# A hybrid decoder block on one core: causal mask added on VectorE with the row's extreme, input stage and scan reordered

## The chip, the cores and the metric

One core of a Trainium2 chip. The metric is the device time of one execution in microseconds (us), given as the median of several runs. Engines are named as in the profile: PE (TensorE, matrix products), PEld (its weight loads), DVE (VectorE), ACT (ScalarE), POOL (GpSimd), SP (SyncE, which here issues most DMA transfers, in a queue of its own that keeps their order).

## What is computed

One decoder layer for 512 tokens of width 1024, in f32. One projection of the normalised input feeds a Mamba-2 scan (SSD, 32 heads in 4 groups, chunks of 128) and a latent attention (16 heads); both are gated and merged. A cross-attention to 256 memory rows and a mixture of 32 experts follow. Of the parts that the change touches the reference reads:

```python
u = rms_norm(h, norm_mix)                     # x * rsqrt(mean(x*x) + 1e-6) * gain
z, xbc, dt_raw, q_a, c_kv, k_rope, gate_ssd, gate_mla = split_cols(u @ w_in, IN_SPLITS)
...
y = ssd_chunked_scan(xh, dt, a, bm, cm)
y = y + d_skip[:, None] * xh
...
sc = einsum('bqhd,bkhd->bhqk', qi, k) * 96 ** -0.5      # queries in blocks of 128
sc = where(kpos[None, :] <= qpos[:, None], sc, -inf)    # causal
o = einsum('bhqk,bkhd->bqhd', softmax(sc), v)
```

## The kernel before

Everything is one function, `block`. Each f32 product with a weight is made of three: the activations lie in SBUF as a high part and a rest (`uh`, `ul`), each weight tile of 128x1024 is split on its arrival into `WHt` (a copy on ACT, L149) and `WLt` (a subtraction on DVE, L150), and `mm3` (L118 to L126) issues the products of high and high, of the rest with `WHt`, and of high with `WLt`, each in 8 steps of 128 rows: 24 PE instructions with 512 columns per output tile. The weights come through `wraw` (L131) in SP's queue into a tag with two buffers.

Input stage (L202 to L255, in a `manual_schedule`, where instructions stay in the order in which they are written): four token tiles `xt[t]` of 128x1024 are loaded; PE is kept busy by 50 identity products (`keep_warm`); ACT squares each tile and sums it (L231); DVE makes the reciprocal roots for two tiles at a time (`mean_rsqrt`, L79 to L109, an integer start and three steps); the tiles are scaled in place (L234 and L243 on DVE, L237 and L244 on ACT); the narrow weights `wd` are split (L241, L246); PE transposes all 32 blocks (L251); ACT and DVE make `uh` and `ul` out of PSUM (L253, L254). Then PE starts with the narrow product (L121, k by k) and the latent projections.

All else is put in order by a list scheduler in the tile framework; pools of buffers (tag `tmp` with four, PSUM tags A and B with four banks each) hold instructions back until a buffer is free. SP's queue holds in order the weight loads, two strided loads of `d_skip` into `dsk` (L313, 64x16 elements of 4 bytes each), the load of the rope table's first two columns `fr` (L570), the rows of the convolution, `dtb` and `ea` (L112).

The scan: `project(g)` gives six output tiles of the projection for group g, with a convolution on each (`conv`, L378 to L389: one ACT and three DVE operations, a tanh, a product). `scan(g)` (L413 to L478) is a generator: one step with the scores of the chunks and the transposes of B, four with transposes of `y` (L431) and products of states (L440), and four for pairs of heads, whose decay rows come back from DRAM as broadcasts (`ac_d`). `drive(a, b, na, nb)` interleaves two generators, na steps of a to nb of b:

```python
    for g in range(3):
        drive(scan(g), project(g + 1), 9, 6)
    drive(scan(3), gate(0), 9, 5)
```

The attention runs in pairs of heads. `stage1` makes query and key, high and rest; `stage2` (L695 to L718) makes the scores of 4 query blocks for both heads in three products each (L706 to L708), a fourth product `identb` x `mQ` (L709) adds -1e30 above the diagonal, DVE takes the negated row maximum from PSUM (L711), ACT takes the exponential from PSUM to SBUF with the row sum (L712), DVE normalises (L713, L718). `stage3` transposes the result on PE (L730), `stage4` multiplies with v. A PSUM bank holds one or two score blocks, and the next ones can have it when the exponentials have read it.

## Time and profile before

| | us |
|---|---|
| median of 3 runs | 1193.38 |
| lowest and highest | 1190.51, 1193.88 |
| profiled execution | 1194.35 |
| its span in the trace | 1192.6 |
| PE busy, in 5972 instructions | 1164.2 |
| PE weight loads | 861.9 |
| DVE busy, in 1500 instructions | 730.8 |
| ACT busy, in 1010 instructions | 517.2 |
| POOL busy | 99.6 |

The granted clock of PE over the whole span is 0.992 of full speed. Weight loads overlap with products. Products of PE are pipelined: a row's duration is longer than the step from one to the next, so the cost of an instruction on PE is read from the starts. An idle time stands in square brackets with what ended it.

## The change

Five parts.

1. Input stage: the root is made for each token tile by itself (ACT square with the mean's factor, ACT root with the epsilon as bias, four small DVE operations, the scaling on DVE), and PE's transposes of a tile stand right behind it. The transposition of the gains (`gcol`) moves to the third tile. `qa0`, the first split of latent weights, is taken after the fourth `uh`/`ul`. A root on a constant has ACT load its table at the start; later the exponential of `a_log` needs a load of its own (7 table loads in the program, before 6).
2. `d_skip`: one broadcast load of 128 rows of 32 (`dsr`) behind the rows of the convolution, and two DVE copies, take the place of the two strided loads.
3. `fr` and `perm`, two loads, become one (`frp`, 128x130), late; two tiles of the same tag grow to 130 columns.
4. Scan: both generators are started by a step each before `drive`.
5. Attention: queries are scaled by the negative factor; `hide`, a bf16 tile with 0 and 1e30, is added to the negated scores by one DVE operation that writes the sum to SBUF and keeps its minimum (`tensor_tensor_reduce`); ACT takes the exponential of what lies in SBUF with scale -1. The 64 mask products and `identb` are gone.

```diff
-    for t in range(NT):
-        junk = tmp([128, D], BF, name="junk")
-        A.activation(junk, xt[:, t], AF.Square, accum_out=ss[:, t:t + 1])
-        if t == 1:
-            rs = mean_rsqrt(sb.tile([128, 2], F32, name="va", tag="rsv", bufs=4), ss[:, :2], 2, 1.0 / D, "rx")
-            V.tensor_scalar(xt[:, 0], xt[:, 0], rs[:, 0:1], None, op0=OP.mult)
-    T.transpose(pu[7][:, :n2], rows2[:n2], ident[:n2, :n2])
-    V.tensor_copy(gcol[:, :n2], pu[7][:, :n2])
-    A.activation(xt[:, 1], xt[:, 1], AF.Copy, scale=rs[:, 1:2])
+    rx = const([128, 4, NT], name="rx")
+    epsx = const([128, 1], name="epsx")
+    V.memset(epsx, EPS)
+    A.activation(rx[:, 0, :1], epsx, AF.Sqrt)
     wdh, wdl = wsplit([128, KD, 96])
     wdc = ((0, 0, 64), (64, 48, 16), (80, 32, 16))
+    for t in range(NT):
+
+        q = slice(t, t + 1)
+        rt, y, v, r = (rx[:, i, q] for i in range(4))
+        junk = tmp([128, D], BF, name="junk")
+        A.activation(junk, xt[:, t], AF.Square, scale=1.0 / 32, accum_out=ss[:, q])
+        A.activation(rt, ss[:, q], AF.Sqrt, bias=epsx)
+        V.tensor_scalar(v, ss[:, q], EPS, -0.5, op0=OP.add, op1=OP.mult)
+        V.reciprocal(y, rt)
+        V.tensor_scalar(v, y, v, y, op0=OP.mult, op1=OP.mult)
+        V.tensor_scalar(r, v, 1.5, y, op0=OP.add, op1=OP.mult)
+        V.tensor_scalar(xt[:, t], xt[:, t], r, None, op0=OP.mult)
+        if t == 2:
+            T.transpose(pu[7][:, 384:384 + n2], rows2[:n2], ident[:n2, :n2])
+            V.tensor_copy(gcol[:, :n2], pu[7][:, 384:384 + n2])
+        for d in range(KD):
+            T.transpose(pu[d][:, t * 128:(t + 1) * 128], xt[:, t, d * 128:(d + 1) * 128], ident)
     for o0, i0, n in wdc:
         A.activation(wdh[:, :, o0:o0 + n], wd[:, :, i0:i0 + n], AF.Copy)
-    rs = mean_rsqrt(sb.tile([128, 2], F32, name="vb", tag="rsv", bufs=4), ss[:, 2:], 2, 1.0 / D, "rx")
-    V.tensor_scalar(xt[:, 3], xt[:, 3], rs[:, 1:2], None, op0=OP.mult)
-    A.activation(xt[:, 2], xt[:, 2], AF.Copy, scale=rs[:, 0:1])
     for o0, i0, n in wdc:
         V.tensor_sub(wdl[:, :, o0:o0 + n], wd[:, :, i0:i0 + n], f(wdh[:, :, o0:o0 + n]))
-    it_q = parts(w_in, 0, C_QA, QL, lo=G)
-    qa0 = next(it_q)
-    for t in range(NT):
-        for d in range(KD):
-            T.transpose(pu[d][:, t * 128:(t + 1) * 128], xt[:, t, d * 128:(d + 1) * 128], ident)
     for d in range(KD):
         A.activation(uh[:, d], pu[d], AF.Copy, scale=gcol[:, d:d + 1])
         stt(ul[:, d], pu[d], gcol[:, d:d + 1], f(uh[:, d]), OP.mult, OP.subtract)
+        if d == 3:
+            it_q = parts(w_in, 0, C_QA, QL, lo=G)
+            qa0 = next(it_q)
...
     dsk = const([128, 16], name="dsk")
     ds_ = I["d_skip"]
+    dsr = tmp([128, 16, 2], name="dsr")
+    row_bcast(dsr.rearrange("p j s -> p (j s)"), ds_, 32)
     for s in range(2):
-        nc.sync.dma_start(dsk[s * 64:(s + 1) * 64],
-                          bass.AP(tensor=ds_.tensor, offset=ds_.offset + s, ap=[[0, 64], [2, 16]]))
+        V.tensor_copy(dsk[s * 64:(s + 1) * 64], dsr[s * 64:(s + 1) * 64, :, s])
...
-    for g in range(3):
-        drive(scan(g), project(g + 1), 9, 6)
-    drive(scan(3), gate(0), 9, 5)
+    for g in range(NG):
+        sc, nx = scan(g), project(g + 1) if g < 3 else gate(0)
+        next(sc)
+        next(nx)
+        drive(sc, nx, 8, 5 if g < 3 else 4)
...
-    fr = const([128, 2], name="fr")
-    nc.sync.dma_start(fr, I["freq"][:, :2])
-    perm = sb.tile([128, 128], F32, name="perm", tag="dec")
-    nc.sync.dma_start(perm, I["freq"][:, 2:])
+    frp = sb.tile([128, 130], F32, name="frp", tag="dec")
+    nc.sync.dma_start(frp, I["freq"])
+    fr, perm = frp[:, :2], frp[:, 2:]
...
-    Pq = slot(2, [128, 3, 1280], name="Pq")
+    S2 = slot(2, [128, 4096], name="S2t")
+    Pq = S2[:, :3840].rearrange("p (s n) -> p s n", s=3)
+
+    hide = S2[:, 3840:].bitcast(BF)
+    V.memset(hide[:, :384], 0.0)
+    V.tensor_scalar(hide[:, 384:], mQ, -1.0, None, op0=OP.mult)
...
-    scale = 96 ** -0.5
+    scale = -96 ** -0.5
...
                 T.matmul(dst, Ql[:96, s, qs], Kh[:96, s, :n], start=False, stop=False)
-                T.matmul(dst, Qh[:96, s, qs], Kl[:96, s, :n], start=False, stop=False)
-                T.matmul(dst[:, n - 128:], identb, mQ, start=False, stop=True)
+                T.matmul(dst, Qh[:96, s, qs], Kl[:96, s, :n], start=False, stop=True)
                 mx = sm[:, 0, s, qc:qc + 1]
-                V.reduce_max(mx, dst, axis=AX.X, negate=True)
-                A.activation(P[:, ROFF[qc]:ROFF[qc] + n], dst, AF.Exp, bias=mx, accum_out=sm[:, 1, s, qc:qc + 1])
+                w = P[:, ROFF[qc]:ROFF[qc] + n]
+                V.tensor_tensor_reduce(w, hide[:, 512 - n:], dst, 1.0, 3e38, OP.add, OP.min, accum_out=mx)
+                A.activation(w, w, AF.Exp, scale=-1.0, bias=mx, accum_out=sm[:, 1, s, qc:qc + 1])
```

SP's queue at the start, before (`wr` are weights, `rows` those of the convolution):

```order
L220 DMA wd<-in_w_in_dram 128x8x32 x2
L131 DMA wr<-in_w_in_dram 128x8x256
L313 DMA dsk<-in_d_skip_dram 64x16x1 x2
L570 DMA fr<-in_freq_dram 128x2
L131 DMA wr<-in_w_in_dram 128x8x128
L131 DMA wr<-in_w_in_dram 128x8x256
L131 DMA wr<-in_w_in_dram 128x8x128 x2
L131 DMA wr<-in_w_in_dram 128x8x256 x2
L308 DMA rows<-in_conv_w_dram 96x128
L309 DMA rows<-in_conv_b_dram 24x128
L112 DMA dtb<-in_dt_bias_dram 128x32
L112 DMA ea<-in_a_log_dram 128x32
L131 DMA wr<-in_w_in_dram 128x8x128
```

And now:

```order
L218 DMA wd<-in_w_in_dram 128x8x32 x2
L129 DMA wr<-in_w_in_dram 128x8x256
L129 DMA wr<-in_w_in_dram 128x8x128
L129 DMA wr<-in_w_in_dram 128x8x256
L129 DMA wr<-in_w_in_dram 128x8x128 x2
L129 DMA wr<-in_w_in_dram 128x8x256 x2
L313 DMA rows<-in_conv_w_dram 96x128
L314 DMA rows<-in_conv_b_dram 24x128
L110 DMA dsr<-in_d_skip_dram 128x32
L110 DMA dtb<-in_dt_bias_dram 128x32
L110 DMA ea<-in_a_log_dram 128x32
L129 DMA wr<-in_w_in_dram 128x8x128
```

The loads of `dsk` and `fr` no longer stand between the weight loads; `dsr` stands behind the rows of the convolution. Line numbers differ by some, as the file is longer.

PE at the start of the scan of group 0, before (`pcb` and `pbt` are the scores and the transposes of B, `pxt` the transposes of `y`, `pa` the products of the projection of group 1):

```order
L420 MATMUL pcb<-S8t 128x128 x4
L424 MATMUL pbt<-ident,S8t 128x128 x3
L431 MATMUL pxt<-ident,y_540 128x128
L126 MATMUL pa<-uh,WHt 128x512 x8
L431 MATMUL pxt<-ident,y_540 128x128
L126 MATMUL pa<-ul,WHt 128x512 x2
L431 MATMUL pxt<-ident,y_540 128x128
L126 MATMUL pa<-ul,WHt 128x512 x6
L126 MATMUL pa<-uh,WLt_76 128x512 x8
L431 MATMUL pxt<-ident,y_540 128x128 x3
```

And now:

```order
L426 MATMUL pcb<-S8t 128x128 x4
L430 MATMUL pbt<-ident,S8t 128x128 x3
L124 MATMUL pa<-uh,WHt 128x512 x8
L124 MATMUL pa<-ul,WHt 128x512 x8
L124 MATMUL pa<-uh,WLt_74 128x512 x8
L437 MATMUL pxt<-ident,y_524 128x128 x6
```

The first six transposes of `y` stand together behind 24 products; before, the first came ahead of them all and the second behind 8.

DVE at the scores of one pair of heads, before:

```order
L645 TENSOR_TENSOR WLt_76<-wkv,WHt 128x512 x2
L711 TENSOR_REDUCE sm<-psc 128x1 x8
L713 RECIPROCAL sm<-sm 128x8
L718 TENSOR_SCALAR Pq<-Pq,sm 128x128
L718 TENSOR_SCALAR Pq<-Pq,sm 128x256
```

And now (an operation with an accumulator shows as two instructions, the second reads it):

```order
L657 TENSOR_TENSOR WLt_74<-wkv,WHt 128x512 x2
L723 ISA S2t,sm<-S2t,psc 128x512
L723 ISA sm 128x1
L723 ISA S2t,sm<-S2t,psc 128x384
L723 ISA sm 128x1
L723 ISA S2t,sm<-S2t,psc 128x512
L723 ISA sm 128x1
...
L723 ISA sm 128x1
L725 RECIPROCAL sm<-sm 128x8
L730 TENSOR_SCALAR S2t<-S2t,sm 128x128
```

Eight reductions become eight masked operations with a read each. On PE the same place loses the loads of `identb` and the mask products; from the end of the attention on, the order is the same on all engines.

## Rows read from the trace of the kernel before

**Rows 1.** The page, part 1: busy us (share of the span) xinstructions.
```profile
PE 1164.2 (98%) x5972; PEld 861.9 (72%) x5972; DVE 730.8 (61%) x1500; ACT 517.2 (43%) x1010; POOL 99.6 (8%) x117
```
**Rows 2.** Waits of PE: what for, us in total, times, longest.
```profile
PE pxt L431 <- DVE y L55: 3.0, 1, 3.0
PE pa L126 <- ACT WHt L149: 2.5, 1, 2.5
...
PE pst L440 <- POOL S6t L435: 0.6, 1, 0.6
```
**Rows 3.** Waits of PE's weight loads.
```profile
PEld psc L706 <- ACT Pq L712: 5.4, 12, 0.8
```
**Rows 4.** Timeline, 0 to 36 us: start, duration, engine, line, out<-in, [idle before <-releaser].
```profile
9.55 0.19 ACT L231 ACTIVATION_READ_ACCUMULATOR junk<-xt 128x1 f32 x1
...
9.84 0.66 PE L251 MATMUL pa<-ident,xt 128*128 128x128 f32 x4
...
10.83 0.66 PE L251 MATMUL pa<-ident,xt 128*128 128x128 f32 x4
...
14.96 2.40 ACT L253 ACTIVATE uh<-pa,gcol 128x512 fp32r<-128x512 f32 x4
...
15.66 2.73 DVE L55 SCALAR_TENSOR_TENSOR ul<-pa,gcol,uh 128x512 fp32r<-128x512 f32 x4 [1.76 <-ACT uh L253]
...
16.46 0.47 PE L121 MATMUL pa<-uh,WHt 128*96 128x512 f32 x1 [1.22 <-DVE ul L55]
```
**Rows 5.** Chain of waits up to 45 us: start, duration, what.
```profile
11.30 4.42 SPq L570
...
15.90 18.59 DMA wr<-in_w_in_dram
```
**Rows 6.** The page, part 6: DMA issues, KB each, us to landing.
```profile
wr<-in_w_in_dram SPq DMA_DIRECT2D x26, 1024.0 KB, 5.4
```
**Rows 7.** Windows: us, busy of PE, PEld, DVE, ACT, POOL, PE clock, DMA share, GB/s.
```profile
22.12:27.54 5.42, 5.42 (x25) 4.49 (x24) 1.23 (x1) 1.54 (x2) 0.00 (x0) 1.00 0.05 0
93.00:95.80 2.80, 0.00 (x0) 0.00 (x0) 2.80 (x5) 2.80 (x6) 0.00 (x0) 0.94 0.35 123
95.80:99.30 3.50, 3.50 (x10) 2.76 (x11) 3.21 (x5) 0.00 (x1) 0.00 (x0) 0.56 0.00 0
592.00:625.00 33.00, 32.81 (x203) 24.27 (x202) 25.07 (x52) 24.83 (x63) 3.90 (x8) 1.00 0.27 80
```
**Rows 8.** Lines by form, whole kernel: busy, mean ns | idle before.
```profile
L55 DVE SCALAR_TENSOR_TENSOR y<-pa,cols,y 128x509 f32<-128x509 f32 x16 | 11.7, 745 | 1.4 <-ACT y L383 1.4
...
L711 DVE TENSOR_REDUCE sm<-psc 128x1 f32<-128x512 f32 x16 | 11.0, 689 | 8.6 <-PE psc L709 8.6
...
L711 DVE TENSOR_REDUCE sm<-psc 128x1 f32<-128x128 f32 x16 | 4.7, 291 | 9.7 <-PE psc L709 9.0 <-ACT Pq L712 0.6
...
L55 DVE SCALAR_TENSOR_TENSOR rxo<-rxt,rxo 128x1 f32<-128x1 f32 x8 | 1.1, 156 | 0.0
...
L712 ACT ACTIVATION_READ_ACCUMULATOR Pq<-psc,sm 128x1 f32 x64 | 13.0, 203 | 0.0
...
L592 ACT ACT_TABLE_LOAD x1 | 1.3, 1283 | 0.0
```
**Rows 9.** Timeline, 86 to 106 us, start of the scan.
```profile
91.62 1.06 ACT L149 ACTIVATE WHt<-wr 128x1024 fp32r<-128x1024 f32 x1 [4.34 <-DMA wr<-in_w_in_dram]
...
95.80 0.47 PE L431 MATMUL pxt<-ident,y 128*128 128x128 f32 x1 [2.98 <-DVE y L55]
...
103.34 0.44 PE L431 MATMUL pxt<-ident,y 128*128 128x128 f32 x2
```
**Rows 10.** Timeline, 592 to 612 us, scores of one pair of heads.
```profile
599.83 0.23 PE L709 MATMUL psc<-mQ,identb 128*128 128x128 bf16 x1
...
599.87 0.48 PE L706 MATMUL psc<-qk 96*128 96x512 f32 x1
...
603.04 0.19 PEld L706 LDWEIGHTS psc<-qk 96*128 96x128 f32 x1 [0.53 <-ACT Pq L712]
```

## What it is predicted to do

> **What bounds the kernel now.** I read the page's busy table first, then what each engine waited for, then the timeline around each wait that the change can touch. TensorE (PE) is busy for 1164.2 of 1192.6 us [rows 1], and the order of the rest of the program after the attention is the same on every engine in both kernels. So the end moves by as much as PE's work up to the end of the attention gets shorter, and a saving on another engine counts only where PE waits for it. The waits of PE in the stages that the change touches are short and few: one of 3.0 us for `y` at L431 (start of the scan of group 0), one of 2.5 us for a weight split at L126, one of 0.6 us at L440 (scan of group 3) [rows 2]. A fourth place is the first product at 16.46 [rows 4], and a fifth the PSUM banks of the attention scores: the weight loads of L706 wait 5.4 us in 12 places for the exponential L712 [rows 3].

> **A. Start of the program.** Before, each token tile is squared on ACT, the reciprocal root is a chain of VectorE (DVE) operations for two tiles at once, and tile 2 is scaled last. The fourth square's sum is read at 9.55, the uh/ul products begin at 14.96 and 15.66, and PE starts at 16.46 [rows 4]. The change gives each tile its own short chain (an ACT root, four small DVE operations, the scaling), and PE transposes a tile as soon as it is there. Eight transposes take 10.83 - 9.84 = 0.99 us [rows 4]. The warm-up ends at about 9.65, so 32 transposes and that of the gains would end at 9.65 + 4.2 = 13.85, and the first of the eight banks is complete 7 transposes, 0.9 us, earlier: 13.0. Is the last tile there in time? Its sum now comes some 0.5 us later than 9.55, as a small root stands behind each square on ACT (about 0.15 to 0.2 us each; the nearest rows are the 0.19 us read and the 0.156 us small DVE operation [rows 4, 8]). With a root, four operations of about 0.16 and 0.75 us of scaling that gives about 11.8, and PE comes to this tile at 12.8: it is. Then uh 0.6 us (four in 2.40), ul 0.7 us (four in 2.73), and hand-over: first product at about 14.65 instead of 16.46. Gain **1.8 us**. Ends: 1.0 if ACT's splits of `wd` stand in the way, 2.7 if ul is ready the sooner. The weight split of qa0, moved behind the fourth uh, costs ACT 1.06 us in the middle of the uh; the fifth uh then comes at about 17.2, and PE at its 0.69 us per k wants it at 17.4. I count nothing.

> **B. The strided loads of `d_skip` and the load of `fr`.** The chain of waits up to 36 us runs through SP's queue: `fr` takes 4.42 us there, the load of the weights that stands behind it is issued at 15.90 and lands 18.59 us later, at 34.49 [rows 5], and only then can ACT split them; a load of twice that size lands in 5.4 us otherwise [rows 6]. While the load hangs, the DMA engines are 5% busy and move 0 GB/s [rows 7]: 2048 pieces of four bytes are ahead of it. PE runs dry and waits 2.5 us [rows 2]. In the change nothing stands between the weights in SP's queue; the load goes out when `wd` is split, at about 14, and lands by 20, while PE wants it at about 20.3 + 5.5 = 25.8. The new `dsr` load is 128 plain rows; it stands behind two weight loads that PE does not need at once, and the two copies on DVE have until the end of the first scan. Waiting for its buffer (the `tmp` pool) it could hold `dtb` and `ea` behind it on SP; they feed the decay chain, which PE takes 11 products (2.5 us) later than before, and the first decay row is needed only in the scan. `frp`, late now, is needed 300 us later. Gain **2.5 us**, with 0 as the other end if the load still comes late.

> **C. Start of the scan.** Before, PE gives out the transposes of `y` (L431) one at a time; the second stands behind 8 products, its source is not ready, and PE idles from 92.8 to 95.8 [rows 2, 9]. DVE and ACT are both busy without a break in 93.0 to 95.8 [rows 7], because ACT had waited 4.34 us for weights [rows 9] and all that stands behind that split came late. [...] So the place costs 3.0 + 1.5 = 4.5 us. In the change both generators are started ahead of the interleaving, and 24 products stand ahead of the first six transposes, 16 more than the second had: 3.6 us, against the 3.0. Next late is the fourth tile of `y`: before, its two transposes come at 103.34 [rows 9]; now 32 products and six transposes are ahead of them, which is about 98.9 in the old count. I went through the new orders of ACT and DVE from the weight load on with the durations of the old rows. With the load landing 1.6 us sooner (one broadcast less shares the queue with it) the tile is ready at about 99.7, so 0.6 to 0.8 us of new wait. Gain 4.5 - 0.6 = **3.9 us**. The decay chain and the broadcasts of its rows, a weight load later each, feed work that PE needs only at L471, behind all the transposes of the scan. Ends: 0 (the wait moves there or stays) and 4.5.

> **D. Scan of group 3.** Four of twelve transposes now follow eight products, before the state product that waited for GpSimd. Gain **0.6 us**.

> **E. Attention.** Removed: 64 mask products. From the start of one to that of the next product is 599.87 - 599.83 = 0.04 us [rows 10], so 64 x 0.04 = 2.6 us of PE. The bank is now freed by DVE's operation and no longer by ACT's exponential. Those waits cover 5.4 us at most [rows 3], of which part hides under the product before; in the row at 603.04 the load waits 0.53 us [rows 10]. I take half, 2.7 us. Added: the reduction on 128x512 (0.689 us) becomes a masked copy with a minimum. The trace has no such operation. The nearest rows are the two-source operation with a PSUM source, 0.745 for 509 elements, so +0.06, and for the accumulator's separate read, which the order shows, 0.156 (smallest DVE operation) to 0.203 (ACT's read) [rows 8], so +0.18: together 0.24 x 64 = 15 us of DVE in 117 us. DVE is 25.07 us busy in the 33.00 us that two pairs of heads take [rows 7]; 8 such steps a pair add 3.8 to that, and it still has 4 us to spare. But a bank waits for its own operation, so some of it shows: I take a quarter, 3.8 us. Sum **2.6 + 2.7 - 3.8 = 1.5 us**. Ends: +8.0 (all the waits go, nothing shows) and -5 (no wait gained, half of the 15 us shows). The exponential now reads SBUF and the table load added on ACT (1.28 us [rows 8]) falls where ACT waits for weights; the two hide tiles are written once, long before. Nothing for these.

> **The sum** is 1.8 + 2.5 + 3.9 + 0.6 + 1.5 = 10.3 us. The profiled execution took 1194.35 us (span 1192.6), 0.97 above the median of the runs, 1193.38; I expect 1184.0 for such an execution and **1183.1 us** as the median.

> **The rivals.**
> - *The bank waits were the bound of the attention.* For it: all 12 waits are for ACT. Against it: PE is 32.81 of 33.00 us busy there [rows 7]. Then E gives 8.0: 1193.4 - 16.8 = 1176.6. Chance 0.12.
> - *The stall of the scan stays or moves.* For it: the decay chain is later and ACT and DVE have the same work. Without C: 1193.4 - 6.4 = 1187.0. Chance 0.12.
> - *The new DVE step shows in every bank.* E gives -5: 1193.4 - 3.8 = 1189.6. Chance 0.07.
> - *Slower: DVE becomes the bound of the attention.* It would be so if the masked step, which reads two sources and keeps an accumulator, ran at half rate. The two ends of the reduction rows give (689 - 291) / 384 = 1.04 ns per element [rows 8]; one such time more for each of 1280 elements of a head, two heads, is 2.65 us a pair, and eight reads of 0.2 make 4.25. It decides from 4.0 us a pair on, where 25.07 + 2 x 4.0 fills the 33 us. It costs 3 us if only the excess over 33 counts and 31 if none is covered (8 x 4.25 - 2.6); with 15 in the middle the time is 1193.4 - 8.8 + 15 = 1199.6. Against it: the two-source operation with a PSUM source costs the same per element as the reduction does [rows 8]. [...] Chance 0.09.
> - The forecast itself: 0.60.

> **How the numbers follow.** A difference under 0.3% (3.6 us) can't be told from none: faster means below 1189.8, slower above 1197.0. Forecast, first and second rival are faster (0.84), the third lies on the edge, and half of it goes to either side; of the slower rival, which reaches from 1188 to 1216, two thirds lie above 1197. With 0.02 of it faster as well that is 0.89 faster, 0.05 same, 0.06 slower; the bounds of A, B and C can add up to a smaller gain, too, so I take 0.83, 0.10 and 0.07. The range goes from the first rival, 1176.5, to just past the third, 1190; what it leaves out is the slower rival and the far ends of A and E, under 2 in 10.

> **What would show it.** Right: first product near 14.7; no wait at L124 for the split near 33; no wait for `y` at the first L437 and a granted clock of 1.00 through 95 to 99; two pairs of the attention in about 32.5 us instead of 33, with DVE near 29 us of them and no wait of the score loads for ACT. Wrong: a masked step of over 1.2 us at 512, a wait of PE for DVE at the scores, or a new wait at the first py of the scan.

## The result and the profile after

| | before | changed |
|---|---|---|
| median of 5 runs, us | 1193.38 | 1177.73 |
| lowest and highest | 1190.51, 1195.96 | 1177.29, 1178.26 |
| span of the profiled execution | 1192.6 | 1175.9 |
| ratio, with its 95% interval | | 0.9871 (0.9855 to 0.9887) |

The change makes the kernel 15.65 us faster; 10.3 were forecast, and the time lies in the range of 1176.5 to 1190. The page's first part for the changed kernel, to be held against [rows 1]:

```profile
PE 1153.3 (98%) x5908; PEld 855.5 (73%) x5908; DVE 730.6 (62%) x1554; ACT 517.2 (44%) x1014; POOL 98.1 (8%) x117
```

PE does 64 instructions less and is busy for 10.9 us less. The waits of PE in the changed kernel (what for, us in total, times, longest), against [rows 2]:

```profile
PE prg L513 <- DVE rgo L55: 1.0, 2, 0.5
PE pa L119 <- DVE ul L55: 0.8, 1, 0.8
...
PE prn L300 <- DVE rqo L55: 0.7, 1, 0.7
...
PE py L477 <- DVE S8t L467: 0.6, 1, 0.6
```

The three waits of [rows 2] are gone. What is left at the places of the change are waits of 0.6 to 1.0 us, of which two are new (`prn`, `prg`: the roots of norms that DVE makes). The start of the program (start, duration, engine, line, operation, tiles, [idle before <-releaser]), against [rows 4]:

```profile
9.65 0.19 ACT L238 ACTIVATION_READ_ACCUMULATOR junk<-xt 128x1 f32 x1
...
13.09 2.42 ACT L255 ACTIVATE uh<-pa,gcol 128x512 fp32r<-128x512 f32 x4 [1.34 <-PE pa L249]
...
13.81 2.73 DVE L55 SCALAR_TENSOR_TENSOR ul<-pa,gcol,uh 128x512 fp32r<-128x512 f32 x4
...
14.62 0.47 PE L119 MATMUL pa<-uh,WHt 128*96 128x512 f32 x1 [0.80 <-DVE ul L55]
```

The fourth square is summed 0.1 us later than before, and yet PE starts with the products at 14.62 instead of 16.46. The start of the scan, against [rows 9]:

```profile
77.08 0.38 SPq L129 DMA_DIRECT2D wr<-in_w_in_dram  x1
...
85.62 1.06 ACT L147 ACTIVATE WHt<-wr 128x1024 fp32r<-128x1024 f32 x1 [3.44 <-DMA wr<-in_w_in_dram]
...
92.22 0.82 PE L437 MATMUL pxt<-ident,y 128*128 128x128 f32 x6
...
94.83 0.44 PE L437 MATMUL pxt<-ident,y 128*128 128x128 f32 x2
```

Six transposes of `y` follow the 24 products at 92.22 without a wait, two more at 94.83. The same places in windows (us; busy of PE, PEld, DVE, ACT, POOL; granted clock; DMA share; GB/s), against [rows 7]:

```profile
20.27:25.69 5.42, 5.42 (x25) 4.49 (x24) 1.22 (x1) 1.54 (x2) 0.00 (x0) 1.00 0.21 46
91.00:94.00 3.00, 3.00 (x18) 2.54 (x17) 2.96 (x5) 2.01 (x3) 0.00 (x0) 1.00 0.00 0
94.00:97.00 3.00, 3.00 (x15) 2.21 (x14) 3.00 (x6) 0.00 (x0) 0.82 (x1) 1.00 0.49 133
```

The step of the products is the same (5.42 us for 24); through the start of the scan the clock stays at 1.00, where it was 0.56 for 3.5 us. And the forms of the attention's new operations (busy, mean ns | idle before), against [rows 8]; they were read from 534 to 645 us, which holds 14 of the 16 operations of each form:

```profile
L724 ACT ACTIVATE S2t<-S2t,sm 128x512 f32<-128x512 f32 x14 | 10.1, 719 | 0.1
...
L723 DVE CUSTOM_DVE_ANT_0 S2t<-S2t,psc 128x512 f32<-128x512 bf16 x14 | 9.6, 686 | 6.8 <-PE psc L720 6.1
...
L723 DVE DVE_READ_ACCUMULATOR2_ANT sm<- 128x1 f32 x56 | 4.7, 83 | 0.0
...
L723 DVE CUSTOM_DVE_ANT_0 S2t<-S2t,psc 128x128 f32<-128x128 bf16 x14 | 4.0, 285 | 2.9 <-PE psc L720 2.9
```

The masked operation takes 686 ns where the reduction took 689, and the read of its accumulator 83 ns. The exponential takes 719 ns from SBUF, where before it took 689 from PSUM (all 16 of the kernel before):

```profile
L712 ACT ACTIVATE Pq<-psc,sm 128x512 f32<-128x512 f32 x16 | 11.0, 689 | 2.6 <-DVE sm L711 2.6
```

**Where the time came from.** In both programs PE issues the same 5908 products, if the 64 mask products are left out, and at most points of the program in the same order. So the start of the n-th product, counted from the first, shows how far one execution is ahead of the other there (worked out from the starts of the trace's rows; us):

| product | place | before | changed | ahead by |
|---|---|---|---|---|
| 120 | latent projections | 25.05 | 23.20 | 1.9 |
| 200 | behind the wait for the split | 46.02 | 41.34 | 4.7 |
| 420 | start of the scan of group 0 | 90.73 | 87.00 | 3.7 |
| 480 | its first state products | 108.37 | 99.63 | 8.7 |
| 1250 | scan of group 3 | 249.23 | 240.69 | 8.5 |
| 1700 | behind the gates | 338.44 | 330.65 | 7.8 |
| 2340 | ahead of the attention | 484.26 | 475.31 | 9.0 |
| 3300 | behind the attention | 668.48 | 650.77 | 17.7 |
| 4620 | router | 920.98 | 903.84 | 17.1 |
| 4740 | routing | 937.46 | 921.79 | 15.7 |
| 5900 | end of the experts | 1176.58 | 1160.06 | 16.5 |

The start (to 480) gives 8.7 us, the attention 8.8, and a little is lost in the scan of group 3 and at the routing.

## The experiments

Each kernel was timed in five rounds beside the kernel before. All ratios are to that kernel; the changed kernel has 0.9871 (0.9855 to 0.9887). 0.001 is 1.2 us.

**1. The attention alone, and all but the attention.** `attn_only` is the kernel before with part 5:

```diff
-                T.matmul(dst[:, n - 128:], identb, mQ, start=False, stop=True)
...
-                V.reduce_max(mx, dst, axis=AX.X, negate=True)
-                A.activation(P[:, ROFF[qc]:ROFF[qc] + n], dst, AF.Exp, bias=mx, accum_out=sm[:, 1, s, qc:qc + 1])
+                w = P[:, ROFF[qc]:ROFF[qc] + n]
+                V.tensor_tensor_reduce(w, hide[:, 512 - n:], dst, 1.0, 3e38, OP.add, OP.min, accum_out=mx)
+                A.activation(w, w, AF.Exp, scale=-1.0, bias=mx, accum_out=sm[:, 1, s, qc:qc + 1])
```

> The kernel before with part 5 alone (the masked operation on DVE, no mask products). Counting the products of PE in both traces, the changed kernel is 9.0 us ahead when the attention starts and 17.7 us at its end, so the attention gave 8.7 us. If the parts add up: 1193.4 - 8.7 = 1184.7 us. If the attention gains only what the forecast said (1.5) and the rest is a matter of how it meets the earlier parts: about 1191.9.

Measured: 1185.86 us, ratio 0.9929 (0.9917 to 0.9942), which is 8.5 us. `no_attn` is the changed kernel with the opposite edit:

> The changed kernel with the attention of before (mask products, reduction and exponential from PSUM). If the parts add up: 1177.7 + 8.7 = 1186.4 us. If the attention is worth 1.5: 1179.2.

Measured: 1185.66 us, ratio 0.9923 (0.9910 to 0.9935): 9.2 us from the other parts. From product 2340 to 3300, the attention, the four kernels take 184.2 (before), 175.3 (`attn_only`), 184.0 (`no_attn`) and 175.5 us (changed). So the attention is worth 8.6 to 8.9 us in either surrounding, six times what was forecast. The two parts together would give 17.7 us and give 15.4; the difference does not arise in the attention (see the routing, below).

**2. The mask products put back.** The changed kernel with a product of zeros where each mask product was:

```diff
-                T.matmul(dst, Qh[:96, s, qs], Kl[:96, s, :n], start=False, stop=True)
+                T.matmul(dst, Qh[:96, s, qs], Kl[:96, s, :n], start=False, stop=False)
+                T.matmul(dst[:, n - 128:], hide[:, :128], hide[:, :128], start=False, stop=True)
```

> The changed kernel with 64 products of zeros put back where the mask products were, each with its weight load; nothing else differs. If the gain is the time of PE for these products: at the 0.04 us step that the forecast read, 64 x 0.04 = 2.6, 1180.3 us; if a product with its weight load costs PE more than that step shows, up to 8.7, 1186.4. If they hide under waits for a bank: 1177.7.

Measured: 1182.44 us, ratio 0.9901 (0.9886 to 0.9915), about 3.6 us slower than the changed kernel. In its profiled execution it is 6.0 us behind at the end of the attention (product 3300), of which 1.1 us were there before the attention began, and gets 3.1 us back in the routing stage, which the edit does not touch.

**3. The exponential from PSUM.** The changed kernel, with the exponential on the unmasked scores and with a constant in place of the row's minimum (it leaves out the mask):

```diff
-                A.activation(w, w, AF.Exp, scale=-1.0, bias=mx, accum_out=sm[:, 1, s, qc:qc + 1])
+                A.activation(w, dst, AF.Exp, scale=-1e-3, bias=ones[:, 0:1], accum_out=sm[:, 1, s, qc:qc + 1])
```

> The changed kernel, but the exponential reads the scores in PSUM again, unmasked and with a small factor (the mask does not reach the output), so that the bank comes free only when ACT is done. If the earlier release of the bank carries the gain: 5 us or more slower, 1183 or above. If it is the mask products alone: 1177.7, or a little less, since ACT's exponential from PSUM took 0.689 us and the one from SBUF takes 0.719.

Measured: 1181.44 us, ratio 0.9892 (0.9878 to 0.9907), about 2.5 us slower. The whole attention as one window in the kernel before, from product 2340 to product 3300 (columns as in [rows 7]):

```profile
484.26:668.48 184.22, 183.05 (x1026) 138.63 (x1024) 120.31 (x241) 115.75 (x267) 17.88 (x36) 1.00 0.27 83
```

In the changed kernel with the products of zeros:

```profile
476.42:656.75 180.33, 179.87 (x1026) 139.57 (x1024) 120.06 (x305) 117.28 (x267) 17.92 (x36) 1.00 0.29 85
```

With the exponential from PSUM:

```profile
475.71:654.10 178.39, 177.68 (x962) 135.97 (x961) 119.87 (x305) 115.18 (x267) 17.92 (x36) 1.00 0.29 86
```

And in the changed kernel:

```profile
475.31:650.77 175.46, 174.86 (x962) 136.18 (x960) 119.55 (x305) 115.37 (x267) 17.91 (x36) 1.00 0.29 87
```

The first column after the bounds is the length: 184.2, 180.3, 178.4 and 175.5 us. The products of zeros cost 4.9 us, or 76 ns for each of the 64, and the later release 2.9. DVE is busy for 120 us in all four. The waits of PE's weight loads for a bank, against [rows 3]; with the exponential from PSUM:

```profile
PEld psc L718 <- ACT S2t L724: 4.9, 15, 0.5
```

And in the changed kernel:

```profile
PEld psc L718 <- DVE sm L723: 2.7, 10, 0.6
```

The releaser is ACT where the exponential reads PSUM and DVE where it does not, and the waits halve.

**4. The scan loop undone.** The changed kernel with the loop of before (part 4 taken out):

```diff
-    for g in range(NG):
-        sc, nx = scan(g), project(g + 1) if g < 3 else gate(0)
-        next(sc)
-        next(nx)
-        drive(sc, nx, 8, 5 if g < 3 else 4)
+    for g in range(3):
+        drive(scan(g), project(g + 1), 9, 6)
+    drive(scan(3), gate(0), 9, 5)
```

> The changed kernel with the scan loop of before (part 4 undone). The trace of the changed kernel gains 5.0 us between the products 420 and 480 (start of the scan) and loses 0.75 around the scan of group 3. If the order of the transposes is the cause: the wait for y and the low clock come back, 4.3 us slower than the changed kernel, at a ratio of about 0.991 to before. If the late weights were the cause, which parts 1 and 2 have mended: no change, ratio 0.987.

Measured: 1177.60 us, ratio 0.9865 (0.9850 to 0.9880): no slower than the changed kernel. Its timeline at the start of the scan:

```profile
77.01 0.38 SPq L129 DMA_DIRECT2D wr<-in_w_in_dram  x1
...
86.30 1.06 ACT L147 ACTIVATE WHt<-wr 128x1024 fp32r<-128x1024 f32 x1 [4.20 <-DMA wr<-in_w_in_dram]
...
90.47 0.33 PE L437 MATMUL pxt<-ident,y 128*128 128x128 f32 x1 [0.77 <-DVE y L55]
```

With the old order the second transpose waits 0.8 us and not 3.0. At product 480 this kernel is 1.0 us behind the changed one (100.66 against 99.63), and at product 1700 it is level with it (330.66 against 330.65).

**5. The new loop for groups 0 to 2 only.** The scan of group 3 and the first gate are interleaved as before:

```diff
-    for g in range(NG):
-        sc, nx = scan(g), project(g + 1) if g < 3 else gate(0)
+    for g in range(3):
+        sc, nx = scan(g), project(g + 1)
         next(sc)
         next(nx)
-        drive(sc, nx, 8, 5 if g < 3 else 4)
+        drive(sc, nx, 8, 5)
+    drive(scan(3), gate(0), 9, 5)
```

> The changed kernel with the new loop for groups 0 to 2 and the old one for group 3 and the first gate. If the new order of group 3 costs (PE waits 1.0 us for the gate's root at prg there, the state product's wait of 0.6 us is gone): 0.75 us faster than the changed kernel in that stretch, ratio 0.9865. If the waits come from the gate itself and not from the order: 0.6 us slower there.

Measured: 1177.83 us, ratio 0.9866 (0.9851 to 0.9881). The time can't be told from the changed kernel's. PE's waits there:

```profile
PE pst L446 <- POOL S6t L441: 0.6, 1, 0.6
```

From product 1250 to 1700 it takes 89.2 us, the kernel before 89.2 and the changed kernel 90.0: the 0.75 us are the new order's. The wait of 0.6 us for GpSimd is back, and those at `prg` (1.0 us) are gone.

**6. Both loads put back, and each alone.** `old_loads` is the changed kernel with parts 2 and 3 undone:

```diff
-    row_bcast(dsr.rearrange("p j s -> p (j s)"), ds_, 32)
     for s in range(2):
-        V.tensor_copy(dsk[s * 64:(s + 1) * 64], dsr[s * 64:(s + 1) * 64, :, s])
+        nc.sync.dma_start(dsk[s * 64:(s + 1) * 64],
+                          bass.AP(tensor=ds_.tensor, offset=ds_.offset + s, ap=[[0, 64], [2, 16]]))
...
-    nc.sync.dma_start(frp, I["freq"])
+    nc.sync.dma_start(fr, I["freq"][:, :2])
...
+    nc.sync.dma_start(perm, I["freq"][:, 2:])
```

> The changed kernel with the two strided loads of d_skip and the early load of the table's two columns back in SP's queue (parts 2 and 3 undone). If the pieces of four bytes hold the weights up: PE waits 2.5 us or more for the split again, a product step near 31 us is missing, and the end comes 2.5 to 4.5 us later, ratio 0.9895 to 0.991. If the new input stage has the loads earlier and so hides them: no change, 0.987.

Measured: 1187.50 us, ratio 0.9937 (0.9923 to 0.9950), 7.9 us slower than the changed kernel, more than either theory had. `dsk_strided` undoes the first half of that edit alone:

> The changed kernel with the two strided loads of d_skip back, the table's load late as in the change. If the 2048 pieces of 4 bytes are the cause: a wait of 2.5 to 5 us for the split and a ratio of 0.992 to 0.994, as with both loads back. If both loads were needed to do the harm: 0.987.

Measured: 1184.81 us, ratio 0.9923 (0.9909 to 0.9936), 6.2 us slower than the changed kernel. `fr_early` undoes the second half alone:

> The changed kernel with the small load of the table's two columns (128 pieces of 8 bytes) back at its early place in SP's queue, d_skip as in the change. If d_skip's pieces of 4 bytes were what held the weights up: no wait for the split, ratio 0.987 as for the changed kernel. If the 4.42 us of this load in the queue were it: the wait is back, ratio 0.990 or more.

Measured: 1176.83 us, ratio 0.9854 (0.9837 to 0.9870): nothing lost. In the trace with the strided loads alone, the chain of waits (start, duration, what) has the weight load again, against [rows 5]:

```profile
14.42 20.32 DMA wr<-in_w_in_dram
```

And PE's wait behind it:

```profile
35.92 3.78 PE L124 MATMUL pa<-uh,WHt 128*128 128x512 f32 x8 [3.84 <-ACT WHt L147]
```

With the early load of `fr` alone, the row of that load is short:

```profile
8.91 0.99 SPq L578 DMA_DIRECT2D fr<-in_freq_dram  x1
```

So most of the 4.42 us that `fr` took in the queue before [rows 5] are gone where `d_skip`'s strided loads do not stand ahead of it. These alone are enough to hold up the weights, which land after 20.3 us. Beside them `fr` is not without effect: with both loads back the weight load goes out at 15.85 instead of 14.42,

```profile
15.85 20.61 DMA wr<-in_w_in_dram
```

and the ratio is 0.0014 (1.7 us) higher than with the strided loads alone, though the intervals overlap.

**7. The new loads alone.** The kernel before with parts 2 and 3:

```diff
-    for s in range(2):
-        nc.sync.dma_start(dsk[s * 64:(s + 1) * 64],
-                          bass.AP(tensor=ds_.tensor, offset=ds_.offset + s, ap=[[0, 64], [2, 16]]))
+    dsr = tmp([128, 16, 2], name="dsr")
+    row_bcast(dsr.rearrange("p j s -> p (j s)"), ds_, 32)
+    for s in range(2):
+        V.tensor_copy(dsk[s * 64:(s + 1) * 64], dsr[s * 64:(s + 1) * 64, :, s])
...
-    fr = const([128, 2], name="fr")
-    nc.sync.dma_start(fr, I["freq"][:, :2])
...
+    nc.sync.dma_start(frp, I["freq"])
```

> The kernel before with parts 2 and 3 alone (d_skip as one broadcast behind the convolution's rows, the table's two loads as one, late). If these loads were the cause of both waits of the start, the one for the split (2.5 us) and the one for y with the low clock behind it (4.5 us): 7 to 8 us faster than before, ratio 0.9935. If only the first: 2.5 us, ratio 0.998.

Measured: 1187.46 us, ratio 0.9939 (0.9925 to 0.9952), 7.3 us faster than before. At product 480 it is 5.6 us ahead, and still 5.6 at product 4620; in the profiled executions another 1.7 us come from the routing stage, where the kernels do not differ. SP's rows near the start of the scan and PE's transposes:

```profile
77.89 0.33 SPq L368 DMA_DIRECT2D ac_d<-acT  x1
...
78.69 0.38 SPq L131 DMA_DIRECT2D wr<-in_w_in_dram  x1
...
79.53 0.33 SPq L112 DMA_DIRECT2D S6t<-ac_d  x1
...
80.62 0.37 SPq L131 DMA_DIRECT2D wr<-in_w_in_dram  x1
...
92.62 0.33 PE L432 MATMUL pxt<-ident,y 128*128 128x128 f32 x1 [0.90 <-DVE y L55]
```

In the kernel before, the same place on SP's queue:

```profile
77.78 0.33 SPq L367 DMA_DIRECT2D ac_d<-acT  x1
...
79.41 0.80 SPq L112 DMA_DIRECT2D S6t<-ac_d  x2
...
81.32 2.32 SPq L131 DMA_DIRECT2D wr<-in_w_in_dram  x2
```

Before, two broadcasts of decay rows (`S6t`) go out ahead of the two weight loads, the first of which comes 3.5 us behind `ac_d`. With the new loads the first weight load stands ahead of the broadcasts and goes out 0.8 us behind `ac_d`. The scan loop is that of before in both kernels. The wait for `y` falls from 3.0 to 0.9 us, and at 92 to 100 us no wait of 3 us is left. The two places in all kernels that bear on them (us between the starts of two products):

| kernel | loads of `d_skip` and `fr` | scan loop | 120 to 200 | 420 to 480 |
|---|---|---|---|---|
| before | old | old | 21.0 | 17.6 |
| `new_loads` | new | old | 18.1 | 14.1 |
| `old_scan` | new | old | 18.1 | 14.0 |
| changed | new | new | 18.1 | 12.6 |
| `fr_early` | `fr` old | new | 18.1 | 13.0 |
| `dsk_strided` | `d_skip` old | new | 24.6 | 14.3 |
| `old_loads` | old | new | 25.6 | 16.3 |

With either set of loads the new loop gains 1.3 to 1.4 us from 420 to 480, and with either loop the new loads gain 3.5 to 3.7 us.

**8. The old input stage.** The changed kernel with part 1 undone:

```diff
-    for t in range(NT):
...
-        A.activation(rt, ss[:, q], AF.Sqrt, bias=epsx)
...
+        if t == 1:
+            rs = mean_rsqrt(sb.tile([128, 2], F32, name="va", tag="rsv", bufs=4), ss[:, :2], 2, 1.0 / D, "rx")
...
```

> The changed kernel with the input stage of before (part 1 undone). If the start's 1.85 us are passed on to the end: first product at 16.5, ratio 0.9887. If a later wait (the one for the root of q at 60 us, or the scan's) takes them up: 0.987.

Measured: 1177.94 us, ratio 0.9865 (0.9850 to 0.9880). No loss can be seen in the time. In its profiled execution PE is 1.6 us behind the changed kernel at product 120, 2.6 at 480, 3.2 at 3300 and 1.6 at 5900, so there the loss is carried into the last stage. The two were not timed against each other, and the intervals leave room for 1.5 us. How far the new stage is ahead also differs from one execution to the next, by up to 1.45 us (step A below), so one trace of each kernel does not give its worth.

**9. Filling the routing stage.** The changed kernel with

```diff
-    keep_warm(34)
+    keep_warm(44)
...
-    keep_warm(8)
+    keep_warm(13)
```

> The changed kernel with more identity products in the two gaps of the routing stage (44 for 34 and 13 for 8), so that PE does not idle there. From product 4620 to 4740 the kernels took 14.8, 16.5 or 17.9 us, and the long ones show a low granted clock behind the gap. If the gap brings the clock down: 14.8 us or less in this stretch, 1.5 to 3 us less than the changed kernel's, ratio 0.9845 to 0.986. If the steps come from something else, or the products only delay what follows: 0.987 or more.

Measured: 1177.01 us, ratio 0.9850 (0.9834 to 0.9866). The stage in the changed kernel, as a window:

```profile
911.20:921.00 9.80, 9.15 (x59) 8.95 (x60) 7.29 (x24) 0.00 (x0) 4.22 (x6) 0.65 0.41 125
```

and with the filled gaps:

```profile
912.00:922.00 10.00, 9.48 (x90) 8.75 (x88) 7.91 (x26) 0.00 (x0) 4.21 (x6) 1.00 0.44 137
```

The clock is 0.65 there in the one and 1.00 in the other. The 44 products that wait for the gathered rows take, in the changed kernel,

```profile
914.69 7.70 PE L75 MATMUL pw<-ident 128*128 128x128 f32 x44
```

and with the filled gaps

```profile
915.46 5.02 PE L75 MATMUL pw<-ident 128*128 128x128 f32 x44
```

The expectation for the stage holds: the stretch takes 14.8 us up to the product that is number 4740 in the changed kernel. That the filling is the cause is not shown, for `mix_scan`, `mask_back`, `no_attn` and `new_loads` take 14.8 us there without it. Nor is it shown whether the kernel gains by it. Its interval overlaps that of the changed kernel, and `fr_early`, timed in the same session without the filling, came to 0.9854. The loads of the experts' weights come next. From the first product of the token gather (`ptk`) to the last product of PE the profiled executions of all fourteen kernels differ by 2.4 us at most, although the stretch up to the first expert product alone differs by 2.7: what the routing loses is in part got back behind it.

## Why the prediction came out as it did

The sign and the range were right; the gain was 15.65 us and not 10.3. The time lies 1.2 us inside the lower end of the range, nearer to the first rival (1176.6) than to the forecast (1183.1), and the stages came in another order of size: the attention, put fourth, gave the most. By its steps:

- **A (1.8 us) has its size, 1.9 at product 120, in part by luck.** The first product came at 14.62 where 14.65 was forecast, and the moved split caused no stall, but two errors cancel. The warm-up, which the forecast let end at 9.65, ended at 9.03; and the last tile, of which it said "it is" in time (ready at 11.8), was ready at 12.7, because DVE's copy of the gains, which stands ahead of that tile's root, waits for PE. PE idles 0.74 us for the tile:

```profile
1.40 7.63 PE L75 MATMUL pa<-ident 128*128 128x128 f32 x50 [1.40 <-DVE ident L61]
...
11.00 0.20 DVE L247 COPY gcol<-pb 128x37 f32<-128x37 f32 x1 [0.63 <-PE pb L246]
...
12.72 0.66 PE L249 MATMUL pa<-ident,xt 128*128 128x128 f32 x4 [0.74 <-DVE xt L244]
```

  Before, the same 50 warm-up products take longer:

```profile
1.40 8.25 PE L77 MATMUL pa<-ident 128*128 128x128 f32 x50 [1.40 <-DVE ident L61]
```

  They take 7.2 to 8.6 us in the ten kernels with the new stage, and in each of these the first product comes 5.6 us behind their end, at 14.16 to 15.61. In the four with the old stage it comes at 16.24 to 16.72, whatever the warm-up took. So the stage is worth 0.6 to 2.6 us, as the warm-up goes; what sets the length of the warm-up is not shown. That the gain reaches the end is not shown by the time (experiment 8).
- **B (2.5 us) was right:** 2.8 us between products 120 and 200. What makes the difference is `d_skip`'s two strided loads, which put back alone make that stretch 24.6 us instead of 18.1. The load of `fr`, which held the largest piece of SP's chain in [rows 5], is harmless by itself and adds 1.0 us at this place beside them (experiments 6 and 7).
- **C (3.9 us) had nearly the size, 5.0, and the wrong cause.** In its sum, 3.0 + 1.5, no run shows the 1.5 us for the low clock apart; they were the author's estimate from [rows 7] (3.50 us less 8 steps of 5.42 / 24 and two transposes of 0.12). In their place the traces show two transposes and 8 products in 3.53 us before, at a clock of 0.57, and in 2.12 us in the changed kernel, at 1.00:

```profile
95.80:99.33 3.53, 3.53 (x10) 2.76 (x11) 3.21 (x5) 0.00 (x1) 0.00 (x0) 0.57 0.00 0
```

```profile
94.83:96.95 2.12, 2.12 (x12) 1.78 (x11) 2.12 (x4) 0.00 (x0) 0.78 (x1) 1.00 0.67 180
```

  The step that failed is "24 products stand ahead of the first six transposes, 16 more than the second had: 3.6 us, against the 3.0". The new order is worth 1.3 to 1.4 us here (experiments 4 and 7), while the new loads give 3.5 with the old loop (experiment 7). The 0.6 us that the forecast took off for the fourth tile of `y` did not occur: its transposes stand at 94.83 without a wait. In the changed kernel that wait comes with the old loads, at 1.6 us with those of `d_skip` alone and 1.9 with both (experiment 6; PE's wait in `old_loads`):

```profile
PE pxt L436 <- DVE y L55: 1.9, 1, 1.9
```

  So the early loads cost twice in the kernel before: 2.8 us where PE ran dry at 33 us, and 3.5 at 93 us, where the weights came late. The rival "the stall of the scan stays or moves" had its 1187.0 from this term and did not occur. What remains open is why the weight loads go out later there: the order on SP's queue differs, and the loads also wait for DVE to have split the tiles before them. No run separates the two.
- **D (0.6 us) had the wrong sign.** The wait for GpSimd did go, but the root of the gate came later, and PE waits 1.0 us for it at `prg`: -0.75 us (experiment 5). The forecast did not ask who stands behind the moved products.
- **E (1.5 us) is the large error: 8.8 us.** Two of its terms are measured by runs, the third by rows. The mask products, 2.6 us by the 0.04 us step of [rows 10], cost 4.9 (experiment 2). That step is the commonest and not the mean. Added over all 64, from each mask product's start to the next product's, it is 4.1 us in the trace before and 4.2 in `mask_back` (worked out from the rows), because 9 and 12 of them take 0.06 to 0.42 us. Where the other 0.7 us arise is open. That the products hold up the bank's release does not show: with them PE's weight loads wait for a bank less, 0.8 us and not 2.7:

```profile
PEld psc L718 <- DVE sm L724: 0.8, 1, 0.8
```

  The earlier release was taken at 2.7 us and is worth 2.9 (experiment 3). The added DVE time, for which 3.8 us were taken off, can't be seen: 0.686 us for the masked operation against 0.689, and 0.083 for the read, where 0.06 more and 0.18 were assumed; no run tests it apart. That makes 7.8 of the 8.8 us. In this stretch `mask_back` differs from the kernel before by the release, DVE's operation and the exponential's source alone and is 3.9 us shorter, so these are worth 1.0 us more while the products are there, and 3.9 and 4.9 make up the 8.8. Two pairs of heads take 30.6 us (products 2886 to 3071), 32.9 before, where the forecast had 32.5 instead of 33.
- **The rival with DVE as the bound** is refuted by the same rows: the two-source operation ran at 686 ns for 512 elements, not at 1.22 us. With one source in PSUM and one in bf16 it took as long as the reduction of one source, 689 ns. In the bounds of this rival the excess over 33 us comes to 2.3 us (4 x 0.57), not 3. The first rival (all of the bank's waits and of the mask products, 1176.6 us) came nearest in time, but 2.7 us of waits for a bank are left, and the sum behind it was another.
- **Not foreseen:** the root of q at `prn` (0.7 us at 60 us), and the routing stage, which took 17.9 us instead of 16.5 in the profiled executions. The clock was 0.65 there in the changed kernel (experiment 9).

## What to carry to other kernels

What a load costs can lie behind it in the queue and not in its own row: here two strided loads of 4 KB each cost 6.2 us (experiment 6), at two places some 60 us apart, while in the kernel before their issues took 2.32 us on SP's queue and their landing 22.8:

```profile
8.94 2.32 SPq L313 DMA_DIRECT2D dsk<-in_d_skip_dram  x2
```

```profile
dsk<-in_d_skip_dram SPq DMA_DIRECT2D x2, 4.0 KB, 22.8
```

Before a wait for a late operand is put down to the order of instructions, look up when its weights were issued and landed. A cheap product is priced by putting it back into the faster version, or at least by the sum of its steps over all its rows, not by the step of one row. And a start that fits a forecast to 0.03 us should be looked up in the traces of other kernels with the same stage: here it moved by 1.45 us between them.

## What the chip showed beyond that

```profile
35.70:39.00 3.30, 3.30 (x15) 2.72 (x16) 1.19 (x1) 0.33 (x1) 0.00 (x0) 1.00 0.36 102
```

Behind 3.0 us (the scan, before) it was 0.56 for 3.5 us [rows 7]; behind 5.3 us, with both old loads, it was 0.50 for 3.9 us:

```profile
37.60:41.50 3.90, 3.85 (x9) 3.08 (x10) 2.34 (x2) 2.21 (x3) 0.00 (x0) 0.50 0.36 94
```

In the same trace it fell behind an idle time of 1.9 us as well, the one for the fourth tile of `y`, which ended at 105.16:

```profile
107.00:109.00 2.00, 2.00 (x6) 1.52 (x6) 1.27 (x3) 0.75 (x1) 1.59 (x2) 0.50 0.40 119
```

So the length of the idle time alone does not tell: 1.9 us went with a fall here and 2.5 us did not before.

In the routing stage PE idles 1.3 us in the same place in most of these kernels, from the same instructions; the clock was 0.65 behind it in the changed kernel and 1.00 in `mix_scan`:

```profile
911.00:921.00 10.00, 8.44 (x80) 7.94 (x80) 7.76 (x26) 0.00 (x0) 4.21 (x6) 1.00 0.42 136
```

From product 4620 to 4740 the profiled executions took 14.8 to 15.0, 16.5 or 17.9 us, with nothing in between. Two of these kernels so differ by 3.1 us in a stage that neither of them touches, which is as much as some of the parts above are worth. Why the clock was low behind that idle time in one execution and not in the other is not shown; one execution of each kernel was profiled.
